# A sixth quartered tile in the first feed-forward's second product

## The chip, the cores and the metric

The kernel runs on one core of a Trainium2 chip. The metric is the device time of one execution in microseconds (us). Its engines run side by side and wait for one another through semaphores: PE (TensorE, matrix products, with its weight loads shown apart as PEld), DVE (VectorE), ACT (ScalarE), POOL (GpSimd) and SP (SyncE, which here only issues DMA transfers). In this program ACT, DVE, POOL and SP each go through their own list of instructions in the order in which it was written.

## The reference, cut to what matters

One decoder layer on 512 tokens of 1024 columns, in float32: a half-step feed-forward, a token mixer, and a second half-step feed-forward, each between two RMS norms.

```
x = x + 0.5 * rms_norm(swiglu_ffn(rms_norm(x, norm_pre[0]), ffn1_w_in, ffn1_w_out), norm_post[0])
mixed = token_mixer(rms_norm(x, norm_pre[1]), w_mix_in, ..., w_mix_out)
x = x + rms_norm(mixed, norm_post[1])
x = x + 0.5 * rms_norm(swiglu_ffn(rms_norm(x, norm_pre[2]), ffn2_w_in, ffn2_w_out), norm_post[2])

def swiglu_ffn(x, w_in, w_out):            # w_in 1024 x 5632, w_out 2816 x 1024
    gate, up = jnp.split(x @ w_in, 2, axis=-1)
    return (jax.nn.silu(gate) * up) @ w_out
```

The change lies in `(...) @ w_out` of the first feed-forward.

## The kernel before

**Products in three parts.** Each float32 operand is split into a high part (a cast on ACT, line 294 for weights, 884 for activations) and a low part (a subtraction on DVE, lines 296 and 885). A product is three matmuls: high by high, high by low, low by high.

**The second product.** `ffn_out` takes the 2816 rows of `w_out` in 11 tiles of 256 rows (`PAIRS = 11`), and the 1024 output columns in two halves. Per half it adds up in four PSUM banks `C[u][v]` (u: even or odd chunk of 128 tokens, v: 256 columns). A tile enters in one of two ways:

- plain (line 1004): 4 chunks of 128 tokens by 2 column halves by 6 matmuls, 48 matmuls of 128x256;
- by quarters (`quartered`, `product`, line 1012): a Strassen-Winograd form with 7 products of 6 matmuls, 42 in all. Three products go straight into `C`; four go into banks `M` that all quartered tiles of a half share. After the half's last quartered tile `common` forms four shared terms from `M` (one copy on ACT, line 1039, and four DVE operations), and `add` adds them to `C` (both on line 969).

A quartered tile needs more preparation: a second weight tile with sums of the four quarters, and sums of the quarters of the activations (`h_sums`, line 919, then split into a tile `hs`), besides the quarters' own parts (`h_quarters`, tiles `once` or `xq`). The sums of weights are not computed on an engine: `sums_ahead` copies quarters into a DRAM buffer `f1sums` by three DMAs on SP's queue (lines 938 to 940) and adds to them by three accumulating DMAs on POOL's queue (line 944), and a load reads the result. `make_sums` starts one such set and moves each begun set on by one step; `ffn_in`, the first product, calls it every fifth of its steps, and `ffn_out` on every other tile of the first half.

`QUARTERED` says which tiles are quartered in each half, `OUT` in which order a half takes its tiles, and `LAST` how many tiles at the end of the second half are held back: they are taken chunk by chunk (128 tokens at a time), so that the norm of a chunk can begin while the next is multiplied. In the second half of the first feed-forward that order is 10, 2, 4, 3, 6, 8, 9 and then, chunk by chunk, 0, 1, 7, 5.

```
FIRST = (2, 3, 4, 5, 6, 7, 8, 9)
OUT = {"f1": [list(range(PAIRS)), [10, 2, 4, 3, 6, 8, 9, 0, 1, 7, 5]]}
LAST, APART, TWICE = {"f1": 4, "f2": 2}, (5, 7, 9), (5, 9)
```

**Room.** Split weights have four places (`w`); a place is free when the last matmul of its tile has read it. Activations of this stage have three places (`hs`) and one more for tile 7 in `xq`. The quarters of tiles 5, 7 and 9 have no place of their own: their high part borrows a buffer of the ring `raw`, from which the mixer's first weights are loaded next, and their low part borrows `gpre`, the tile into which the pre-norm's gain for the mixer is loaded next (line 165).

**The end of the stage.** After a chunk's last matmul: `add` where it is due, squares and their sum on ACT (line 453), the root on POOL (lines 454 and 458), the scaling and the addition to `xs` on DVE (lines 501 and 509), then squares and root again for the mixer's norm, the scaling by `gpre` on DVE (line 481), and transposes on PE (line 364). `copies_early` also starts the copies of the second feed-forward's sums (`f2sums`, 7 sets of three DMAs on SP's queue). `head4` begins the mixer's first products (line 560).

**Order.** The program is written in the order of these functions; a scheduler then orders each engine's list by its own estimate of when things are ready.

Of the kernel before, what the change touches and what calls it, by code (L numbers as in the profile page):

```python
# [84 lines left out]


FIRST = (2, 3, 4, 5, 6, 7, 8, 9)
QUARTERED = {"f1": [FIRST, (2, 3, 4, 6, 8)], "f2": [FIRST, (2, 3, 4, 6, 8, 9, 5)]}
OUT = {"f1": [list(range(PAIRS)), [10, 2, 4, 3, 6, 8, 9, 0, 1, 7, 5]]}
OUT["f2"] = [OUT["f1"][0], [10, 2, 4, 3, 6, 8, 9, 5, 7, 0, 1]]  # L90
LAST, APART, TWICE = {"f1": 4, "f2": 2}, (5, 7, 9), (5, 9)
# [3 lines left out]
EVERY, EARLY, AHEAD = 5, 7, 13  # L95
# [28 lines left out]
class Layer:  # L124
    def __init__(self, ctx, tc, aps):
# [23 lines left out]
            (f, h, k2): dram.tile([P, 4, QUARTER], F32, name=f"{f}sums{h}_{k2}")  # L149
            for f in ("f1", "f2") for h in range(2) for k2 in OUT[f][h] if k2 in QUARTERED[f][h]  # L150
        }
# [691 lines left out]
    def ffn_in(self):  # L843

        nc = self.nc
        if not self.second:
            self.begun = ()
            self.sums_due("f1")
        for n, (p, t) in enumerate(ORDER2[len(HEADS2) :] if self.second else ORDER[len(HEADS) :]):
            if n > 14 and n % EVERY == 0 and not self.second:  # L850
                self.make_sums()
            if n == 14 and self.second:

                with self.behind(self.pooled):
                    nc.gpsimd.drain()
            with self.behind(*(self.c22 if p in ("p3", "p5") and self.second else ())):
                self.feed()
            self.c22 = []
            self.lag()
            self.prod(p, t)  # L860
            self.after(p, t)
            if t == PAIRS - 1 and p in ("p3", "p7"):
                self.hs.append(self.h_tile(len(self.hs)))
            if n == 1 and not self.second:
                self.lower_bound()
        self.feed()
        self.lag()
# [96 lines left out]
    def ffn_out(self, gpost_row, scale, after, trans, head):  # L964
# [5 lines left out]
        f = "f2" if self.second else "f1"  # L970
        OF, QF, LF = OUT[f], QUARTERED[f], LAST[f]
        low = self.low
# [234 lines left out]
    def ffn_items(self, name, w_in, w_out):  # L1207
# [47 lines left out]
        for h in range(2):  # L1255
            for k2 in OUT[name][h]:
                src = w_out[k2 * 2 * P : (k2 + 1) * 2 * P, h * 512 : (h + 1) * 512].rearrange("(k p) d -> p k d", p=P)
                key = (name, "out", h, k2)
                four = k2 in QUARTERED[name][h]
                made.append(Item(key, [Load(key, src, 2, 512, "raw2", 5, 8)], sums=four))  # L1260
# [717 lines left out]
```

## Time and profile before

| | us |
|---|---|
| median of 3 runs | 915.35 |
| lowest and highest | 915.20 and 915.37 |
| the profiled execution's own time | 916.13 |
| span in that profile, first to last instruction | 914.4 |
| PE busy in the span | 906.1 |
| DVE, ACT, POOL busy | 767.2, 522.0, 183.7 |

All times of places in the program below are counted from the span's start in the profiled execution. The second product of the first feed-forward lies between about 224 and 339 us; its second half of the columns begins at about 280 us. An engine's busy time says what it did, not whether it was waited for; that is read from the rows of single instructions, where a bracket gives the idle time ahead of an instruction and what ended it.

### The profile page before, as it was taken

To read this page: it belongs to the slowest core of one execution; us is meant where nothing else is said; L and a number is where in the kernel's file an instruction comes from. 1 tells how busy PE (TensorE), PEld (TensorE's weight loads), DVE (VectorE), ACT (ScalarE), POOL (GpSimd) and SP (SyncE) were. 2 spreads that over 40 slices of the span, in tenths; PEclk is the share of its full clock that TensorE was granted. 3 is DMA by queue.
4 is the path that set the end of the run, shared out by engine and by line. 5 is a ranking of instruction groups with operands and counts; after the bars stand their busy time and mean duration, and the time that the engine had idled before them with its cause. 6 is when DMAs were issued, how large, how long until landed. Compare 5 with 4: busy or idle time off the path is not lost.

```text
span 914.4 us, 18150 instructions
## 1 busy us (share of the span) xinstructions
PE 906.1 (99%) x7330; PEld 874.9 (96%) x7330; DVE 767.2 (84%) x1005; ACT 522.0 (57%) x749; POOL 183.7 (20%) x256
## 2 busy tenths in 40 slices
PE   9999999999999999999999999999999999999997
PEld 8999999999999999998888887899999999999997
DVE  6899988889888876799896556799999889998886
ACT  7645545557566567957643345684454545757661
POOL 2541112121111047742230300322000000010002
PEclk9999999999999999999999999999999999999999
DMA  9355779775897815898953126253344445378542
GB/s 306 88 165 136 189 188 216 187 159 138 219 280 233 258 55 144 162 192 207 214 112 109 47 70 213 65 161 102 97 148 139 138 123 159 104 231 246 170 146 93
DMA packets 127921, 146.51 MB, mean 160 GB/s; under 512 B 16335, under 2 KB 100303, under 8 KB 127837
## 3 DMA queue, kind: packets, MB, share of 16 engines
q1 hardware_dynamic: 111868, 130.14, 46.4%
q0 software_dynamic: 15680, 14.69, 11.9%
q8 instruction: 57, 0.93, 0.4%
q10 hardware_dynamic: 288, 0.52, 0.2%
q14 instruction: 28, 0.22, 0.1%
HBM read 143.20 MB, written 31.48 MB: 191 GB/s over the span
## 4 chain that ended last, share of the span: by engine, by line
PE 62%; ACT 0%; DVE 0%; DVEq 0%; POOLq 0%; issue 0%; POOL 0%; ACTq 0%
PE ps L619 23%; PE ps L1012 8%; PE ps L549 6%; PE ps L198 5%; PE ps L200 5%; PE ps L199 5%; PE ps L1004 4%; PE ps L560 1%; PE ps L1441 1%; PE ps L364 1%; PE ps L1540 0%; PE ps L1742 0%; PE ps L1491 0%; PE ps L1715 0%; PE ps L1739 0%; PE ps L1717 0%
## 5 line engine op out<-in xcount | busy, mean ns | idle before, releaser
L294 ACT CAST w<-raw 128x1024 fp32r<-128x1024 f32 x246 | 250.6, 1027 | 192.0 <-PE ps L619 91.1
L296 DVE TENSOR_TENSOR w<-raw,w 128x1024 fp32r<-128x1024 f32 x246 | 299.4, 1221 | 30.3 <-ACT w L294 28.9
L619 PE MATMUL ps<-xq,w 128*128 128x256 f32 x2016 | 237.4, 277 | 0.0
L619 PEld LDWEIGHTS ps<-xq,w 128*128 128x128 f32 x2016 | 233.3, 188 | 0.1
L619 PE MATMUL ps<-sq,w 128*128 128x256 f32 x1512 | 178.0, 276 | 0.0
L619 PEld LDWEIGHTS ps<-sq,w 128*128 128x128 f32 x1512 | 174.6, 188 | 0.0
L310 DVE TENSOR_TENSOR raw<-raw,raw 128x1024 f32<-128x1024 f32 x72 | 89.7, 1252 | 7.5 <-DMA raw<-in_ffn_w_in_dram 6.2
L1012 PE MATMUL ps<-w,hs 128*128 128x256 f32 x672 | 80.9, 276 | 0.0
L1004 PE MATMUL ps<-w,hs 128*128 128x256 f32 x672 | 79.2, 276 | 0.0
L1012 PEld LDWEIGHTS ps<-w,hs 128*128 128x128 f32 x672 | 78.3, 188 | 0.0
L1004 PEld LDWEIGHTS ps<-w,hs 128*128 128x128 f32 x672 | 77.5, 188 | 0.0
L198 PE MATMUL ps<-w,xq 128*128 128x512 f32 x176 | 71.1, 405 | 0.1
L199 PE MATMUL ps<-w,xq 128*128 128x512 f32 x176 | 68.6, 391 | 0.0
L200 PE MATMUL ps<-w,xq 128*128 128x512 f32 x176 | 68.6, 391 | 0.0
L549 PE MATMUL ps<-xq,w 128*128 128x256 f32 x480 | 55.7, 277 | 0.0
L944 POOL DMA_DIRECT2D f2sums<-in_ffn_w_out_dram x15 | 20.0, 1507 | 177.5 <-DMA f2sums<-in_ffn_w_out_dram 177.0
L549 PEld LDWEIGHTS ps<-xq,w 128*128 128x128 f32 x480 | 54.9, 188 | 0.5 <-issue 0.5
L884 ACT CAST hs<-hf 128x1024 fp32r<-128x1024 f32 x32 | 33.7, 1054 | 28.0 <-PE ps L1012 20.3
L885 DVE TENSOR_TENSOR hs<-hf,hs 128x1024 fp32r<-128x1024 f32 x32 | 39.1, 1223 | 9.0 <-ACT hs L884 8.4
L944 POOL DMA_DIRECT2D f1sums<-f1sums x26 | 22.3, 859 | 110.1 <-DMA f1sums<-in_ffn_w_out_dram 56.1
L944 POOL DMA_DIRECT2D f2sums<-f2sums x30 | 26.3, 905 | 87.1 <-DMA f2sums<-in_ffn_w_out_dram 42.4
L310 POOL TENSOR_TENSOR raw<-raw,raw 128x1024 f32<-128x1024 f32 x12 | 32.6, 2724 | 40.9 <-DVE w L296 40.7
(263 smaller groups left out, 1232.9 us busy)
## 6 DMA issues: line engine op xcount, KB each, us to landing
raw<-in_ffn_w_in_dram SPq DMA_DIRECT2D x98, 512.0 KB, 4.7
raw<-in_ffn_w_out_dram SPq DMA_DIRECT2D x44, 512.0 KB, 5.1
raw<-in_w_mix_in_dram SPq DMA_DIRECT2D x28, 512.0 KB, 5.7
raw<-f2sums SPq DMA_DIRECT2D x15, 512.0 KB, 5.2
raw<-f1sums SPq DMA_DIRECT2D x13, 512.0 KB, 7.0
raw<-in_w_mix_out_dram SPq DMA_DIRECT2D x8, 512.0 KB, 4.3
f2sums<-in_ffn_w_out_dram SPq DMA_DIRECT2D x30, 128.0 KB, 5.0
f2sums<-in_ffn_w_out_dram SPq DMA_DIRECT2D x15, 256.0 KB, 6.1
```

What stands on the lines that cost most here:

```text
L198: mm(ps, sh, mh, start=start, stop=False, **kw)
L199: mm(ps, sh, ml, start=False, stop=False, **kw)
L200: mm(ps, sl, mh, start=False, stop=stop, **kw)
L294: nc.scalar.copy(hi, raw)
L296: self.low = nc.vector.tensor_tensor(lo, raw, hi.bitcast(F32), op=ALU.subtract)
L310: added = (nc.vector if late else nc.gpsimd).tensor_tensor(o, o, c, op=ALU.add)
L549: mm(ps[:, u0:u1], w[:, a, k, :], self.xop(k, b, u0, u1), start=k + n + m == 0, stop=k == ND - 1 and n == 2, skip_group_check=True,)
L619: self.nc.tensor.matmul(ps[:, c], wb[b][:, k, v], left[d][:, k, :], start=first and a + n + k == 0, stop=n == 2 and k == KH - 1, skip_grou ...
L885: self.nc.vector.tensor_tensor(lo, src, hi.bitcast(F32), op=ALU.subtract)
L944: nc.gpsimd.dma_start(to[:, a:b], v, accum_op=ALU.add)
L1004: mm(out, a[kk][:, i * P : (i + 1) * P], w[:, b, kk, QUARTER * v : QUARTER * (v + 1)], start=begin and c == kk == n == 0, stop=kk == 1 and ...
L1012: mm(ps[:, QUARTER * c : QUARTER * (c + 1)], A[a][:, c], B[b], start=begin and c == n == 0, stop=n == 2, skip_group_check=True,)
```

## The change

```
-QUARTERED = {"f1": [FIRST, (2, 3, 4, 6, 8)], "f2": [FIRST, (2, 3, 4, 6, 8, 9, 5)]}
+QUARTERED = {"f1": [FIRST, (2, 3, 4, 6, 8, 9)], "f2": [FIRST, (2, 3, 4, 6, 8, 9, 5)]}
...
         for n, (p, t) in enumerate(ORDER2[len(HEADS2) :] if self.second else ORDER[len(HEADS) :]):
-            if n > 14 and n % EVERY == 0 and not self.second:
+            if n > 9 and n % EVERY == 0 and not self.second:
                 self.make_sums()
```

Tile 9 is taken by quarters in the second half of the columns too. With that no plain tile stands any more between the last quartered tile and the four that go chunk by chunk. Its sums of weights are a fourteenth set, and the first set is begun at step 10 of `ffn_in` and no longer at step 15. Since 9 is in `TWICE`, its quarters and sums are prepared anew for the second half, in borrowed places again.

PE, second half of the columns, tile 9 and what follows, before (`hs_3711` is tile 9, `hs_3767` tile 0; `ps_3441` and `ps_3442` are `C[0]`, `ps_3443` and `ps_3444` are `C[1]`):

```order
L1004 MATMUL ps_3441<-w,hs_3711 128x256 x6
L1004 MATMUL ps_3442<-w,hs_3711 128x256 x6
L1004 MATMUL ps_3441<-w,hs_3711 128x256 x6
L1004 MATMUL ps_3442<-w,hs_3711 128x256 x6
L1004 MATMUL ps_3443<-w,hs_3711 128x256 x6
L1004 MATMUL ps_3444<-w,hs_3711 128x256 x6
L1004 MATMUL ps_3443<-w,hs_3711 128x256 x6
L1004 MATMUL ps_3444<-w,hs_3711 128x256 x6
L1004 MATMUL ps_3441<-w,hs_3767 128x256 x6
```

And now, from the third of its seven products on (`once` is tile 9's quarters, `hs_3730` their sums, `hs_3779` tile 0; `ps_3508` to `ps_3510` are three of the banks `M`, `ps_3448` to `ps_3450` banks of `C`):

```order
L1012 MATMUL ps_3450<-w,hs_3730 128x256 x6
L1012 MATMUL ps_3509<-w,hs_3730 128x256 x6
L1012 MATMUL ps_3508<-w,hs_3730 128x256 x6
L1012 MATMUL ps_3510<-w,hs_3730 128x256 x6
L1012 MATMUL ps_3449<-w,once_3720 128x256 x2
L1012 MATMUL ps_3449<-w,once_3721 128x256
L1012 MATMUL ps_3449<-w,once_3720 128x256 x2
L1012 MATMUL ps_3449<-w,once_3721 128x256
L1004 MATMUL ps_3448<-w,hs_3779 128x256 x6
```

Eight groups of six became seven, and the banks `M` are complete only just ahead of tile 0.

DVE at the same place, before (the rows of line 969 are `common` and `add`; `raw_247` and `raw_249` are the weights of tiles 7 and 5, `hs_3774` and `hs_3779` the activations of tiles 1 and 5):

```order
L969 TENSOR_TENSOR hf_113<-ps_3501,hf_113 128x512
L885 TENSOR_TENSOR xq_77<-hf_113,xq_76 128x1024
L969 TENSOR_TENSOR hf_113<-ps_3503,hf_113 128x512
L296 TENSOR_TENSOR w<-raw_247_3634,w 128x1024
L969 TENSOR_TENSOR hf_113<-hf_113,ps_3502 128x512
L885 TENSOR_TENSOR hs_3774<-hf_113,hs_3774 128x1024
L969 TENSOR_TENSOR hf_113<-ps_3501,hf_113 128x512
L969 TENSOR_TENSOR ps_3443<-ps_3443,hf_113 128x512
L969 TENSOR_TENSOR ps_3444<-ps_3444,hf_113 128x512
L885 TENSOR_TENSOR hs_3779<-hf_113,hs_3779 128x1024
L296 TENSOR_TENSOR w<-raw_249_3665,w 128x1024
L969 TENSOR_TENSOR ps_3441<-ps_3441,hf_113 128x512
```

And now (`raw_249` and `raw_250` are the weights of tiles 7 and 5, `hs_3846` the activations of tile 5):

```order
L296 TENSOR_TENSOR w<-raw_249_3672,w 128x1024
L969 TENSOR_TENSOR hf_114<-ps_3508,hf_114 128x512
L969 TENSOR_TENSOR ps_3451<-ps_3451,hf_114 128x512
L969 TENSOR_TENSOR hf_114<-ps_3510,hf_114 128x512
L296 TENSOR_TENSOR w<-raw_250_3694,w 128x1024
L969 TENSOR_TENSOR hf_114<-hf_114,ps_3509 128x512
L885 TENSOR_TENSOR hs_3846<-hf_114,hs_3846 128x1024
L969 TENSOR_TENSOR hf_114<-ps_3508,hf_114 128x512
L969 TENSOR_TENSOR ps_3450<-ps_3450,hf_114 128x512
L969 TENSOR_TENSOR ps_3448<-ps_3448,hf_114 128x512
```

All of line 969 now stands behind the weights of tile 7, and the low part of tile 5's activations stands inside it.

SP's queue, before, where the gain for the mixer's norm is loaded (`gpre`):

```order
L255 DMA raw_191_3290<-f1sums_3_92 128x1024
L255 DMA raw_3736<-in_w_mix_in_dram 128x8x128
L165 DMA gpre_3923<-in_norm_pre_dram 128x1024
L255 DMA raw_196_3327<-in_ffn_w_out_dram 128x2x512
L255 DMA raw_234_3447<-f1sums_6_93 128x1024
```

And now, behind the 21 copies for the second feed-forward, of which these are the last:

```order
L255 DMA raw_3839<-in_w_mix_in_dram 128x8x128
L940 DMA f2sums_6_100<-in_ffn_w_out_dram 128x512
L938 DMA f2sums_7_101<-in_ffn_w_out_dram 128x256
L939 DMA f2sums_7_101<-in_ffn_w_out_dram 128x256
L940 DMA f2sums_7_101<-in_ffn_w_out_dram 128x512
L938 DMA f2sums_8_102<-in_ffn_w_out_dram 128x256
L939 DMA f2sums_8_102<-in_ffn_w_out_dram 128x256
L940 DMA f2sums_8_102<-in_ffn_w_out_dram 128x512
L165 DMA gpre_3938<-in_norm_pre_dram 128x1024
L255 DMA raw_4216<-in_w_mix_in_dram 128x8x128
```

The gain's load went from ahead of all `f2sums` copies to behind all of them, and one load of the mixer's weights went in between them. The sums of tile 9 make one weight load more ahead of the copies.

## Prediction

> **What bounds the kernel now.** I read the page's first part, then busy time by stretch, then PE's waits, then single instructions around the stage's end.
>
> ```profile
> span 914.4 us, 18150 instructions
> PE 906.1 (99%) x7330; PEld 874.9 (96%) x7330; DVE 767.2 (84%) x1005; ACT 522.0 (57%) x749; POOL 183.7 (20%) x256
> ```
>
> PE is busy for 906.1 of 914.4 us, so time is won or lost in PE's work and in PE's few waits. The stretches of the second half of the columns (five quartered tiles, the plain tile 9, the chunks), with PE, PEld, DVE, ACT, POOL in this order:
>
> ```profile
> 285.66:309.46 23.80, 23.80 (x213) 23.80 (x211) 17.37 (x17) 16.44 (x18) 0.00 (x0) 1.00 0.76 235
> 309.46:314.90 5.44, 5.44 (x51) 5.44 (x49) 5.44 (x7) 1.52 (x2) 0.00 (x0) 1.00 0.92 246
> 314.90:336.60 21.70, 21.70 (x193) 21.70 (x192) 15.25 (x25) 10.41 (x29) 6.84 (x17) 1.00 0.34 95
> ```
>
> PE has no gap. DVE is idle for 6.4 us over the five quartered tiles, but never in the 5.44 us of tile 9. PE's matmuls there, and its next wait:
>
> ```profile
> 301.30 2.88 PE L1012 MATMUL ps<-w,hs 128*128 128x256 f32 x24
> 306.06 2.88 PE L1012 MATMUL ps<-w,hs 128*128 128x256 f32 x24
> 309.46 8.32 PE L1004 MATMUL ps<-w,hs 128*128 128x256 f32 x72
> 317.62 1.52 PE L1004 MATMUL ps<-w,xq 128*128 128x256 f32 x12
> 338.79 5.53 PEld L560 LDWEIGHTS ps<-xq,w 128*128 128x128 f32 x48 [0.29 <-ACT w L294]
> ```
>
> From one row to the same place of the next tile a quartered tile takes 306.06 - 301.30 = 4.76 us, and 72 plain matmuls take 317.62 - 309.46 = 8.16 us, 113.3 ns each. PE then runs without a stop up to 338.5, where the mixer's first product waits 0.29 us for a weight cast on ACT. That wait has a history, and it decides this change. The chain of waits ends there with
>
> ```profile
> 336.35 0.47 ACT junk L453 x2
> 336.83 0.96 ACT xq L370 x2
> 337.79 0.95 ACT w L294
> 338.79 5.73 PE ps L560 x48
> ```
>
> and going back from 336.35 instruction by instruction I find no slack:
>
> ```profile
> 319.86 1.38 DVE L969 TENSOR_TENSOR ps<-ps,hf 128x512 f32<-128x512 f32 x2 [1.31 <-PE ps L1004]
> 322.94 0.75 DVE L509 SCALAR_TENSOR_TENSOR xs<-y,col,xs 128x512 f32<-128x512 f32 x1 [0.66 <-POOL col L458]
> 323.79 0.63 ACT L453 ACTIVATE junk<-xs 128x512 f32<-128x512 f32 x1 [1.96 <-DVE xs L509]
> 326.42 1.43 DVE L481 SCALAR_TENSOR_TENSOR xn<-xs,col,gpre 128x512 f32<-128x512 f32 x2 [2.06 <-POOL col L458]
> 329.26 0.64 ACT L453 ACTIVATE junk<-xs 128x512 f32<-128x512 f32 x1 [2.73 <-DVE xs L509]
> 331.89 1.43 DVE L481 SCALAR_TENSOR_TENSOR hf<-xs,col,gpre 128x512 f32<-128x512 f32 x2 [2.06 <-POOL col L458]
> 334.74 0.63 ACT L453 ACTIVATE junk<-xs 128x512 f32<-128x512 f32 x1 [1.80 <-DVE xs L509]
> ```
>
> Each step starts when the one before ends: the addition to `C[0]` at 319.86 lets the first chunk's norm begin; that ends in the scaling by `gpre` at 326.42; behind it on DVE stands the second chunk's addition, whose norm scales at 331.89; behind that the third chunk's, whose squares at 334.74 hold ACT until 336.35. So from 319.86 to 338.79 there is a second path beside PE's, of 18.93 us, and at 338.79 it is the later one by 0.29 us. The stage ends when the addition at 319.86 starts, plus 18.93, unless something delays the chain.
>
> **The change part by part.** *PE's work.* Tile 9 goes from 48 to 42 matmuls: 6 x 113.3 ns = 0.68 us less (5.44 to 4.76). This is the whole possible gain; it brings tile 0 from 314.90 to 314.22.
>
> *When the addition to `C[0]` now starts.* It stands on DVE behind the rest of `common`. The durations and distances come from
>
> ```profile
> 309.76 1.22 DVE L885 TENSOR_TENSOR xq<-hf,xq 128x1024 fp32r<-128x1024 f32 x1
> 310.90 0.68 DVE L969 TENSOR_TENSOR hf<-ps,hf 128x512 f32<-128x512 f32 x1
> 311.50 1.22 DVE L296 TENSOR_TENSOR w<-raw,w 128x1024 fp32r<-128x1024 f32 x1
> 315.10 1.06 ACT L884 CAST hs<-hf 128x1024 fp32r<-128x1024 f32 x1 [4.12 <-PE ps L1004]
> 316.06 1.04 ACT L294 CAST w<-raw 128x1024 fp32r<-128x1024 f32 x1
> ```
>
> A low part of 1024 lets the next start after 1.14, one of line 969 after 0.60; ACT starts 0.20 after PE frees a place (315.10 after 314.90). Tile 9's first weight place is free after 18 matmuls, at 311.50: ACT casts tile 7's weights from 311.70 to 312.75, DVE takes their low part at 312.78. Then 313.92 and three rows of line 969 up to 315.72. Tile 9's sums are read after 36 matmuls (313.54), its second weights at 314.22; ACT casts tile 5's activations 313.74 to 314.80 and its weights 314.70 to 315.75. DVE: their low part at 315.78, line 969 at 316.92, the activations' low part at 317.52 (done 318.74), line 969 at 318.66 and 319.26, and the addition to `C[0]` at 319.86. PE reaches tile 5 in the first chunk at 314.22 + 3 x 1.36 = 318.30 and needs that low part in its third matmul, so it waits some 0.4 us for 318.74; the matmuls that the addition needs end near 319.4, ahead of 319.86. PE would leave the first chunk at 320.05, where it was 320.34.
>
> So PE arrives 0.3 us earlier, but the addition starts at the same 319.86 as before. By the chain the stage ends at 338.79 again, PE waits 0.6 us there in place of 0.3, and the gain is gone: 0.0, with -0.3 if the chain starts that much earlier than I count and -0.68 at most.
>
> *The load of `gpre`.* It was far ahead; now it waits for tile 9 (its buffer) and stands behind the copies. It is needed at 326.42, on the chain without slack.
>
> ```profile
> 275.27 1.58 SPq L165 DMA_DIRECT2D gpre<-in_norm_pre_dram  x1
> 302.93 2.22 SPq L255 DMA_DIRECT2D raw<-in_ffn_w_out_dram  x1
> 305.20 0.51 SPq L938 DMA_DIRECT2D f2sums<-in_ffn_w_out_dram  x1
> 318.76 0.60 SPq L940 DMA_DIRECT2D f2sums<-in_ffn_w_out_dram  x1
> DMA to landing us min/median/max: 4.4/5.1/5.4
> DMA to landing us min/median/max: 3.8/3.8/3.8
> DMA to landing us min/median/max: 7.1/7.1/7.1
> ```
>
> (The landings are those of the `f2sums` copies, of the one load of a gain that the trace shows landing, and of a load of mixer weights at 300 us.) The copies took the queue from 305.20 to 319.36. Now two issues more stand ahead or among them; an issue takes 0.3 to 0.6 when the queue flows and 1.6 to 2.2 behind other large loads, so `gpre` is issued between 320.0 and 323. It lands 3.8 to 7.1 later. Ends: 323.8, which costs nothing, and 330.1, which costs 3.7. I take 321.3 + 5.4, the slowest copy, because it moves among copies: 326.7, late by 0.3.
>
> The Trainium skill, "DMA: Bandwidth & Descriptors", section "Queues, rings and completion order", says that each DMA engine consumes the descriptors of a ring in order. By it `gpre` cannot overtake the eight last copies; by the 3.8 us of a gain's load alone it would land at 325.1 and cost nothing, by the rule at 326.7 or later. No row here shows a load among copies landing early.
>
> *More work for DVE and ACT*: the quarters' low parts, three sums and one more split of 768 columns. The same operations for other tiles:
>
> ```profile
> 246.05 0.69 DVE L919 TENSOR_TENSOR hsum<-hf,hsum 128x512 f32<-128x512 f32 x1
> 257.49 1.02 DVE L885 TENSOR_TENSOR once<-hf,once 128x256 fp32r<-128x256 f32 x2
> 298.42 0.96 DVE L296 TENSOR_TENSOR w<-raw,w 128x768 fp32r<-128x768 f32 x1 [0.27 <-ACT w L294]
> 255.00:300.00 45.00, 45.00 (x399) 45.00 (x399) 37.43 (x47) 29.84 (x47) 6.32 (x13) 1.00 0.85 252
> ```
>
> At most 3 x 0.69 + 1.02 + 0.96 = 4.1 us of DVE, ahead of 305, where DVE is idle for 45 - 37.4 = 7.6 us between 255 and 300: 0. Without that cover it would delay the splits of weights behind it one for one.
>
> *The sums begun earlier.* SP's queue gets three issues more behind 65.83:
>
> ```profile
> 65.83 0.53 SPq L255 DMA_DIRECT2D raw<-in_ffn_w_in_dram  x1
> 75.09 4.97 SPq L255 DMA_DIRECT2D raw<-in_ffn_w_in_dram  x2
> ```
>
> Between them the queue waits for a buffer for 8.7 us; three issues take under 2. All later sets keep the places that other sets had, and the fourteenth ends where the thirteenth did: 0, and 2 at most if the weights behind came late.
>
> Sum: -0.68 (PE) + 0.4 (tile 5) + 0.3 (chain takes the rest) + 0.3 (`gpre`) = +0.3. The profiled execution took 916.13, 0.78 above the median; the difference is applied to the median: 915.35 + 0.3 = 915.65, say 915.7.
>
> **The rivals.** *The gain arrives.* If tile 5's weights or activations are ready earlier, or the addition overtakes, PE keeps 0.3 to 0.68: 914.7 to 915.05. Against it: DVE's continuous row from 312.78 to 319.86.
>
> *`gpre` is late in earnest.* One mechanism, at 326.42: each us of landing after it is a us of time. From 328.25 on (7 us after an issue at 321.3) it makes the kernel slower by over 0.2%: 916.4 to 919. For it: DMA is busy 0.92 in tile 9's stretch and gets three loads more; against it: the copies' landing never exceeds 5.4.
>
> *A stopped PE runs slower afterwards.* The granted clock is 1.00 around the 0.29 us wait:
>
> ```profile
> 338.50:340.00 1.50, 1.41 (x12) 1.21 (x12) 1.35 (x3) 1.42 (x4) 0.54 (x1) 1.00 0.00 0
> ```
>
> With `gpre` at 330.1 PE would stand 0.6 + 3.7 us at 338; if its 48 matmuls of 5.73 us then ran at half speed, 5.7 more: up to 924.8. The Trainium skill, "TensorE: Matmul & The Clock Gate", section "HAM oscillation — how this bites in real kernels", warns of idle gaps above some 3.4 us. No wait here is that long, so the trace cannot confirm it.
>
> *The early sums disturb* the first product's weights: 915.7 to 917.4.
>
> **How the numbers follow.** Chain-bound with `gpre` at most 1 us late: 0.62 (915.2 to 916.4). The gain arrives: 0.15. `gpre` over 1 us late: 0.19, most of it over 1.83. Clock: 0.02. Early sums: 0.02. About 0.2% (1.83 us) is what a measurement of this kernel can tell from no change. Slower by more: 0.13 + 0.02 + 0.01 = 0.16; faster by more: 0.01, since PE's whole saving is 0.68; within: 0.83. The range, 914.9 to 917.5, leaves out the full gain and the latest landings; the likeliest case alone is 915.2 to 916.4.
>
> **What would show it.** Right: 42 matmuls for tile 9 in 4.76 us; a wait of about 0.4 at tile 5 of the first chunk; line 969 on `C[0]` at 319.9; line 481 at 326.4 to 327.4, ended by POOL or by the load of `gpre`; PE's wait at 338.5 of 0.6 us or more. Wrong: line 969 clearly before 319.6 or after 320.5; PE starting the mixer before 338.5; a PE gap between 60 and 280.

## The result and the profile after

The changed kernel takes 920.02 us in the median of 7 runs (919.11 to 925.47), the kernel before 915.37 (915.20 to 915.49): a ratio of 1.0066, with a 95% interval from 1.0053 to 1.0080. It is slower by 4.65 us, and it lies outside the range that was given, 914.9 to 917.5. The seven executions fall into two groups: four between 919.1 and 920.0 and three between 923.6 and 925.5. The profiled one, 919.99 us by its own time, is of the first group.

The page's first part, after:

```profile
span 918.3 us, 18165 instructions
PE 906.7 (99%) x7324; PEld 874.8 (95%) x7324; DVE 770.6 (84%) x1011; ACT 524.0 (57%) x752; POOL 185.9 (20%) x259
```

PE executes 7324 matmuls where it had 7330, six fewer as intended, and yet is busy 0.6 us longer; the span is 3.9 us longer. So PE's work cannot be the whole story: PE waits more, and somewhere its matmuls run slower. PE's waits behind 300 us say where:

```profile
PE ps L560 <- ACT w L294: 2.0, 1, 2.0
PE ps L364 <- DVE hf L481: 0.9, 1, 0.9
PE ps L1004 <- DVE hs L885: 0.2, 1, 0.2
```

Of these, before had only the first, with 0.29 us. Row by row on PE (start, duration, group, and in brackets the idle time ahead and its releaser):

```profile
308.98 1.52 PE L1012 MATMUL ps<-w,once 128*128 128x256 f32 x12
310.34 2.88 PE L1012 MATMUL ps<-w,hs 128*128 128x256 f32 x24
313.74 2.88 PE L1004 MATMUL ps<-w,hs 128*128 128x256 f32 x24
318.42 2.90 PE L1004 MATMUL ps<-w,hs 128*128 128x256 f32 x23 [0.21 <-DVE hs L885]
341.36 7.35 PE L560 MATMUL ps<-xq,w 128*128 128x256 f32 x48 [2.02 <-ACT w L294]
348.55 1.03 PE L364 MATMUL ps<-ident,xn 128*128 128x128 f32 x8
```

Tile 9 begins at 308.98 here (309.46 before: this execution came 0.48 us earlier into the stage) and takes 313.74 - 308.98 = 4.76 us. The 48 first matmuls of the mixer, 5.73 us before, now take 7.35. What PE waited for, on DVE and on SP's queue:

```profile
318.88 1.89 DVE L969 TENSOR_TENSOR ps<-ps,hf 128x512 f32<-128x512 f32 x3
329.00 1.41 DVE L481 SCALAR_TENSOR_TENSOR xn<-xs,col,gpre 128x512 f32<-128x512 f32 x2 [5.12 <-DMA gpre<-in_norm_pre_dram]
305.44 0.51 SPq L938 DMA_DIRECT2D f2sums<-in_ffn_w_out_dram  x1
320.56 0.60 SPq L940 DMA_DIRECT2D f2sums<-in_ffn_w_out_dram  x1
321.72 0.35 SPq L165 DMA_DIRECT2D gpre<-in_norm_pre_dram  x1
```

The scaling by `gpre`, which POOL used to release, is released by the load. The load was issued behind the copies of `f2sums` (305.44 to 321.16) and the scaling starts 7.28 us after its issue. The granted clock, the last column but two of these stretches, is 1.00 up to 342 and then:

```profile
342.00:344.00 2.00, 2.00 (x12) 2.00 (x12) 1.89 (x4) 1.56 (x2) 1.56 (x2) 0.53 0.09 14
344.00:346.00 2.00, 2.00 (x13) 2.00 (x13) 2.00 (x3) 1.48 (x3) 0.66 (x1) 0.61 0.86 248
346.00:348.00 2.00, 2.00 (x20) 2.00 (x20) 2.00 (x3) 1.75 (x4) 1.30 (x2) 1.00 0.25 34
```

PE was busy throughout these rows, with 12 or 13 matmuls in 2 us instead of 20: it did not wait there, it ran at a lower clock. In stretches of 0.2 us the granted clock reads 0.50 from 342.2 to 345.4 and 1.00 again from 345.6 on: some 3.4 us at half clock.

**A ruler for this stage.** Executions enter the stage some tenths of a us apart, so below I measure from the start of tile 9. *Scaling* is the time from there to the first line 481; *stage* is the time to the transposes (line 364) that follow the mixer's first 48 matmuls. Before, the latter stand at

```profile
344.36 1.03 PE L364 MATMUL ps<-ident,xn 128*128 128x128 f32 x8
```

so that before has a scaling of 326.42 - 309.46 = 16.96 and a stage of 344.36 - 309.46 = 34.90. After has 329.00 - 308.98 = 20.02 and 348.55 - 308.98 = 39.57: the scaling is 3.06 us late, the stage 4.67, and 4.67 - 3.06 = 1.61 is the matmuls at lower clock (7.35 - 5.73 = 1.62).

### The profile page after: what moved, and what is told of

Its sections match the earlier page's. It is cut to its first block, busy times and chain, and to the rows that moved or that the text cites. A ratio compares the mean times of both kernels' runs of the same rounds, so it can differ in the third digit from the quotient of the medians.

```text
span 918.3 us, 18165 instructions
## 1 busy us (share of the span) xinstructions
PE 906.7 (99%) x7324; PEld 874.8 (95%) x7324; DVE 770.6 (84%) x1011; ACT 524.0 (57%) x752; POOL 185.9 (20%) x259
## 4 chain that ended last, share of the span: by engine, by line
PE 62%; ACT 0%; issue 0%; DVE 0%; DVEq 0%; POOLq 0%; POOL 0%; ACTq 0%
PE ps L619 23%; PE ps L1012 8%; PE ps L549 6%; PE ps L198 5%; PE ps L200 5%; PE ps L199 5%; PE ps L1004 4%; PE ps L560 1%; PE ps L1441 1%; PE ps L364 1%; PE ps L1540 0%; PE ps L1742 0%; PE ps L1491 0%; PE ps L1715 0%; PE ps L1739 0%; PE ps L1717 0%
## 5 line engine op out<-in xcount | busy, mean ns | idle before, releaser
L294 ACT CAST w<-raw 128x1024 fp32r<-128x1024 f32 (+1 forms) x247 | 251.6, 1027 | 192.4 <-PE ps L619 90.8
L296 DVE TENSOR_TENSOR w<-raw,w 128x1024 fp32r<-128x1024 f32 (+1 forms) x247 | 300.3, 1220 | 29.3 <-ACT w L294 27.8
L1012 PE MATMUL ps<-w,hs 128*128 128x256 f32 x696 | 83.8, 276 | 0.0
L1012 PEld LDWEIGHTS ps<-w,hs 128*128 128x128 f32 x696 | 81.1, 188 | 0.0
L1004 PE MATMUL ps<-w,hs 128*128 128x256 f32 x624 | 74.0, 277 | 0.2 <-DVE hs L885 0.2
L1004 PEld LDWEIGHTS ps<-w,hs 128*128 128x128 f32 x624 | 72.2, 188 | 0.4 <-DVE hs L885 0.4
L944 POOL DMA_DIRECT2D f1sums<-f1sums x28 | 24.7, 883 | 113.9 <-DMA f1sums<-in_ffn_w_out_dram 56.8
```

The source lines that it names most:

```text
L294: nc.scalar.copy(hi, raw)
L296: self.low = nc.vector.tensor_tensor(lo, raw, hi.bitcast(F32), op=ALU.subtract)
L944: nc.gpsimd.dma_start(to[:, a:b], v, accum_op=ALU.add)
L1004: mm(out, a[kk][:, i * P : (i + 1) * P], w[:, b, kk, QUARTER * v : QUARTER * (v + 1)], start=begin and c == kk == n == 0, stop=kk == 1 and ...
L1012: mm(ps[:, QUARTER * c : QUARTER * (c + 1)], A[a][:, c], B[b], start=begin and c == n == 0, stop=n == 2, skip_group_check=True,)
```

## The experiments

Each ratio below compares with executions of the kernel before in the same series; their medians lay between 915.61 and 915.85.

**The early sums alone.** The kernel before, with the second part of the change only:

```
-            if n > 14 and n % EVERY == 0 and not self.second:
+            if n > 9 and n % EVERY == 0 and not self.second:
```

> The kernel before with the first set of sums begun at step 10 of the first product; tile 9 stays plain in the second half. Theory (the late gain load, then the slowed clock): this edit has no part in the loss, 915.2 to 915.6. Rival (the sums begun earlier disturb the weight loads of the first product): 917 to 920, with PE gaps between 60 and 225 us.

Measured: 915.73 us (915.31 to 916.49), ratio 0.9998 [0.9989, 1.0007]. The stage is 34.91 us. The sums begun earlier have no part in it.

**The late load alone.** The kernel before, tile 9 plain, with the load of `gpre` forced behind the last copy, and nine sets of copies ahead of it instead of seven:

```
-EVERY, EARLY, AHEAD = 5, 7, 13
+EVERY, EARLY, AHEAD = 5, 9, 13
...
+        last = self.copies_last if tag == "gpre" else None
+        with self.behind(*([last] if last else [])):
             self.nc.sync.dma_start(g, row.broadcast_to([P, D]))
```

> The kernel before, tile 9 plain, with only the load of the mixer's gain moved behind the copies of the second feed-forward's sums; nine sets of copies stand ahead of it in place of seven, so that it is issued near 323 us and lands near 328.0 to 329.5, where it is needed at 326.4. Theory: the load alone makes the loss: the scaling by the gain starts 1.6 to 3.1 us late, PE stands 1.9 to 3.4 us ahead of the mixer's first product, and where the clock falls after that another 1.6: 917 to 920. Rival (the quartered tile, with common close to the chunks, makes the loss): 915.4, no wait for the gain or one that costs nothing.

Measured: 921.72 us (921.44 to 922.55), ratio 1.0062 [1.0050, 1.0074]. The rows of SP, DVE and PE:

```profile
324.88 0.59 SPq L168 DMA_DIRECT2D gpre<-in_norm_pre_dram  x1
332.75 1.41 DVE L485 SCALAR_TENSOR_TENSOR xn<-xs,col,gpre 128x512 f32<-128x512 f32 x2 [7.84 <-DMA gpre<-in_norm_pre_dram]
345.10 5.16 PE L564 MATMUL ps<-xq,w 128*128 128x256 f32 x43 [2.02 <-ACT w L298]
```

Without any change to tile 9, the late load alone makes a loss of this kind, and here a larger one. It landed later than expected: the scaling starts 7.87 us after the issue, 22.74 us after tile 9's start (310.01), which is 5.78 late, and the time grew by 5.9. (PE's first 43 matmuls ran here at full speed, although it had waited 2.02 us ahead of them and 1.71 and 1.25 before.)

**The load ahead of the copies.** The changed kernel; the load is issued before `copies_early`, whose copies then stand behind it:

```
+            self.gpre1 = self.gain("gpre", self.norm_pre[0][1:2, :])
             self.copies_early()
...
-        w, last = (self.ffn1_w_out, self.ffn2_w_out)[f == "f2"][0], self.loaded1 if early else self.loaded
+        w, last = (self.ffn1_w_out, self.ffn2_w_out)[f == "f2"][0], self.gained if early else self.loaded
```

> The changed kernel with the gain's load moved ahead of the copies: it waits for tile 9 at 314 us and the 21 copies wait behind it. Theory: the gain lands near 320, the scaling by it waits for POOL again, PE's wait ahead of the mixer is some 0.6 us and the clock stays at 1.00: 915.0 to 915.6, since the norm's chain starts where it did before. Rival (the quartered tile makes the loss): 919 to 920 as before.

Measured: 921.13 us in the median, but in two groups: 915.75 to 916.90 (5 executions) and 921.05 to 923.40 (7); ratio 1.0041 [1.0022, 1.0060]. The profiled execution (916.90) is of the first group. In it the stage is whole again:

```profile
315.59 0.53 SPq L165 DMA_DIRECT2D gpre<-in_norm_pre_dram  x1
327.25 1.43 DVE L481 SCALAR_TENSOR_TENSOR xn<-xs,col,gpre 128x512 f32<-128x512 f32 x2 [2.06 <-POOL col L458]
339.62 5.72 PE L560 MATMUL ps<-xq,w 128*128 128x256 f32 x48 [0.27 <-ACT w L294]
```

POOL releases the scaling again; tile 9 began at 310.29, so the scaling is 16.96 and the stage 34.89, the values of before. So the late load, with the fall of the clock behind it, is the whole loss inside the stage, and there is a second loss of some 6 us elsewhere, in seven of the twelve executions.

**A place of its own for tile 9's quarters**, so that `gpre` is not borrowed and is loaded as early as before (line numbers are one higher in this kernel):

```
-                        a = self.h_quarters(k2, PLACES.get(k2))
+                        a = self.h_quarters(k2, AGAIN9 if half and k2 == 9 and not self.second else PLACES.get(k2))
```

with `AGAIN9 = 1`, a place in `xq`.

> The changed kernel with tile 9's quarters of the second half in the place that tile 2 leaves at 290 us, and not in the buffers of the gain and of the mixer's weights: both loads go back to where they stood in the kernel before. Theory: 914.9 to 915.5; PE does 0.68 us less, the addition to C[0] starts where it did, and the norm's chain takes the rest. If the chain were not binding: 914.7. Rival (the quartered tile makes the loss): 919 to 920.

Measured: 916.61 us (915.34 to 922.89; two of twelve at 922.9, the others up to 917.17), above the 914.9 to 915.5 expected; ratio 1.0017 [1.0001, 1.0033]. Load issued at 275.35, scaling 16.96, stage 34.90. The quarters are there, all 42 matmuls, and yet the stage is not shorter by a hundredth.

**The wait filled.** The changed kernel with 12 transposes (1.47 us in its profile) ahead of the mixer's first product, into a bank that it overwrites:

```
+        if t + m == 0:
+            for _ in range(FILLERS):
+                self.nc.tensor.transpose(ps[:, :P], self.ident, self.ident)
```

> The changed kernel, with 12 transposes of the identity (about 1.8 us) ahead of the mixer's first product, into the bank that this product then overwrites. They fill PE's wait of 2.02 us there and change nothing else; the gain's load stays late. Theory (the late load starts it, and the wait of 2.02 us then halves the granted clock, 1.62 us): the wait is covered but for 0.2 us, the clock stays 1.00 from 341 on, the first 48 matmuls of the mixer take 5.7 us again, and the time falls by about 1.6 us, to 918.4. Rival (the slow matmuls have another cause, such as the 0.85 us wait six us earlier, or a fixed rhythm): the clock falls all the same, and the time stays at 920.

Measured: 918.6 us (917.48 to 924.56), ratio 1.0042 [1.0023, 1.0062]; four executions at 917.5 to 918.1, two at 922.9 and 924.6, two between. The profiled execution (920.37) had a later load than after (scaling 20.67, 3.71 late), a stage 3.70 longer, and a clock of 1.00 throughout: the loss is the lateness alone. That speaks for the wait as the cause of the slow matmuls, but it does not prove it, since `b_gain_late` kept its clock without any filling; and the second group blurs the median.

**Fewer copies ahead of the load.** The changed kernel with four sets instead of seven:

```
-EVERY, EARLY, AHEAD = 5, 7, 13
+EVERY, EARLY, AHEAD = 5, 4, 13
```

> The changed kernel with 4 sets of copies for the second feed-forward's sums ahead of the gain's load instead of 7 (12 transfers instead of 21); the other three are made later, in the mixer. Theory (the gain's landing is set by the transfers queued ahead of it): it is issued near 316.5, lands at 322 to 324, before it is needed at 326.4; the scaling ends its wait on POOL again, the mixer's first product on 0.3 us; 915.2 to 916. Rival (each load of the gain that is issued in this stretch takes 10 us and more, whatever stands ahead): still late by 0.5 us or more and 916.5 to 918. If the three sets moved into the mixer cost something there: 1 us more in either case.

Measured: 938.10 us (936.76 to 940.29), ratio 1.0246 [1.0232, 1.0259]: neither theory's number. In the stage it is as the first one had it:

```profile
316.06 0.96 SPq L165 DMA_DIRECT2D gpre<-in_norm_pre_dram  x1
326.39 1.43 DVE L481 SCALAR_TENSOR_TENSOR xn<-xs,col,gpre 128x512 f32<-128x512 f32 x2 [2.06 <-POOL col L458]
338.77 5.71 PE L560 MATMUL ps<-xq,w 128*128 128x256 f32 x48 [0.30 <-ACT w L294]
```

Scaling 16.98, stage 34.91. But the three sets that are now made in the mixer cost there what my expectation had put at 1 us:

```profile
502.06 0.81 POOL L944 DMA_DIRECT2D f2sums<-f2sums  x1 [2.59 <-DMA f2sums<-f2sums]
502.61 1.51 POOL L1624 TENSOR_SCALAR_AFFINE_SELECT e<-e 128x512 f32<-128x512 f32 x2
503.56 1.29 DVE L1634 SCALAR_TENSOR_TENSOR pT<-ps,e 128x512 f32<-128x512 f32 x2 [25.21 <-POOL e L1624]
504.31 1.54 PE L1672 MATMUL ps<-ident,qk 128*128 128x128 f32 x6 [19.48 <-DVE pT L1634]
```

This is a place that the prediction had left out. In the mixer POOL issues the accumulating transfers of `f2sums` (line 944), and most of them wait for the landing of an earlier transfer. Behind that row, on the same engine, stands the selection of line 1624 for the mixer's scores. DVE needs it for line 1634, and PE's line 1672 waits for that. With three sets more the row ends at 502.6, and PE stands for 19.48 us. Here, where PE stood waiting for it, line 1672 started 1.70 us after the selection, so a distance of 1.7 us means no margin. Before, it started 12.0 us after it:

```profile
472.09 0.81 POOL L944 DMA_DIRECT2D f2sums<-f2sums  x1 [3.11 <-DMA f2sums<-f2sums]
472.69 1.51 POOL L1624 TENSOR_SCALAR_AFFINE_SELECT e<-e 128x512 f32<-128x512 f32 x2
484.69 0.87 PE L1672 MATMUL ps<-ident,qk 128*128 128x128 f32 x6
```

By this distance the other profiles read: `a_sums_early` 11.1, after 10.1, `d_own_place` 5.4, `e_filled_wait` 1.7, and `c_gain_first` 1.8:

```profile
483.86 1.51 POOL L1625 TENSOR_SCALAR_AFFINE_SELECT e<-e 128x512 f32<-128x512 f32 x2
485.62 1.09 PE L1673 MATMUL ps<-ident,qk 128*128 128x128 f32 x6
```

Leave aside this kernel and `b_gain_late`, whose five executions lie close together (921.4 to 922.6). Then each kernel so far with executions above 922 is one whose selection started 5.4 us or less ahead of line 1672 in a profile (the changed kernel in its second profile, below).

**After, and the load ahead of the copies, once more for their traces.** No edit in either.

> The changed kernel once more, for its trace. Its times lay at 919 to 920 and at 923.6 to 925.5. Theory: an execution of the second kind has the same late load and, on top of it, a longer stretch at half clock or a later stop at another place, which the trace then shows as 4 to 5 us. Rival: the load itself lands 4 us later in it.

> The changed kernel with the gain's load ahead of the copies once more, for its trace. Its times lay at 915.8 to 916.9 and at 921 to 923.4. Theory: an execution of the second kind has a stop of PE at a place behind 340 us (a weight or a sum that comes late because the copies were moved back by the load), 2 to 6 us with the clock's part. Rival: no new stop, and PE runs at a lower granted clock from some place on.

Measured: 919.46 us and 915.84 us, one run each; neither fell into the second group, so no trace of that group was seen. The second execution of the changed kernel is worth having all the same:

```profile
323.93 0.35 SPq L165 DMA_DIRECT2D gpre<-in_norm_pre_dram  x1
329.80 1.41 DVE L481 SCALAR_TENSOR_TENSOR xn<-xs,col,gpre 128x512 f32<-128x512 f32 x2 [4.90 <-DMA gpre<-in_norm_pre_dram]
342.16 5.73 PE L560 MATMUL ps<-xq,w 128*128 128x256 f32 x48 [2.00 <-ACT w L294]
342.00:344.00 2.00, 1.84 (x16) 1.84 (x17) 1.86 (x3) 2.00 (x5) 1.26 (x2) 1.00 0.00 0
486.45 1.51 POOL L1624 TENSOR_SCALAR_AFFINE_SELECT e<-e 128x512 f32<-128x512 f32 x2
488.17 1.13 PE L1672 MATMUL ps<-ident,qk 128*128 128x128 f32 x6
```

The same wait of 2.0 us as in the first execution, but no fall of the clock: scaling 2.85 late, stage 2.84 longer. And the distance from selection to line 1672, 10.1 in the first execution, is 1.7 in this one: in the same kernel POOL's row, from its first issue to its last, took 103.8 us in one execution and 110.9 in the other. In the second execution with the load ahead of the copies the distance was 2.1 us.

**A shorter row.** The changed kernel, with one set of sums less in the mixer (`AHEAD` 12 instead of 13), and then the same with tile 9's place of its own:

```
-EVERY, EARLY, AHEAD = 5, 7, 13
+EVERY, EARLY, AHEAD = 5, 7, 12
```

> The changed kernel with one set of sums for the second feed-forward less in the mixer (12 instead of 13 done by its end; the thirteenth is made in the second feed-forward). POOL's row of accumulating transfers in the mixer, behind which its selection for the mLSTM scores stands (line 1624), becomes three transfers shorter, about 10 us. Theory (two costs: the late load of the gain, 3 to 4 us in every execution; and in some executions POOL's row reaching past the point where PE needs the scores, 3 to 6 us more): the selection stands 10 us or more ahead of PE's line 1672 again, the executions at 923 to 925 are gone, and all lie at 918.5 to 920.5. Rival (the second group comes from somewhere else): times up to 925 remain.

> The changed kernel with tile 9's quarters in the place of their own (so that the gain's load is early again) and with 12 instead of 13 sets done by the mixer's end. Theory of two costs: both are gone; all executions lie at 915.0 to 916.0 against 915.4 to 915.9 of before, none above 917. Rival (the quarters' 0.68 us do arrive once both are gone): 914.7 to 915.2. Rival (something else of the change costs as well): 916.4 or more.

Measured for the first: 920.39 us (918.25 to 921.17, 6 executions), ratio 1.0046 [1.0033, 1.0059]. The distance is 19.5 us, and nothing lies above 921.2 (918.5 to 920.5 was expected). In the profiled one the scaling is 2.42 late, the stage 4.03 longer; the clock fell again, and 1.61 us are its part, as in the first profile of after:

```profile
341.37 7.35 PE L560 MATMUL ps<-xq,w 128*128 128x256 f32 x48 [2.01 <-ACT w L294]
```

Measured for the second: 915.96 us (915.54 to 918.20, 11 executions), ratio 1.0008 [1.0000, 1.0017]; the distance is 15.9 us and nothing lies at 922 any more. None above 917 was expected; three lie at 917.5 to 918.2, where before had one of 17, at 918.4.

```profile
326.50 1.43 DVE L482 SCALAR_TENSOR_TENSOR xn<-xs,col,gpre 128x512 f32<-128x512 f32 x2 [2.07 <-POOL col L459]
338.88 5.71 PE L561 MATMUL ps<-xq,w 128*128 128x256 f32 x48 [0.30 <-ACT w L295]
344.43 1.03 PE L365 MATMUL ps<-ident,xn 128*128 128x128 f32 x8
```

Tile 9 began at 309.52: scaling 16.98, stage 34.91. With both costs removed the change stands where before stood, 0.2 us above it by the medians. No kernel that was run beats the kernel before.

**Fewer copies and a shorter row.** The changed kernel with `EARLY` 4 and `AHEAD` 10, so that the mixer makes six sets as before. In it the last two sets of sums for the second feed-forward are not completed, so nothing behind 700 us, and no time of the whole, says anything about the change.

> The changed kernel with 4 sets of copies ahead of the gain's load instead of 7, and 10 sets instead of 13 done by the mixer's end, so that the mixer makes six sets as before. Theory: the gain is issued 5 us earlier and lands before 326.4, POOL's row in the mixer ends early, and the time is 915.0 to 916.2 without any change to the places of buffers. Rival (the borrowed buffer costs by itself, whatever is queued): 917 or more, with the scaling of line 481 still ended by the load. If the five sets made late hold up the second feed-forward: a PE wait behind 760 us.

Measured: 921.98 us (918.80 to 924.34), with a PE wait in the second feed-forward,

```profile
PE ps L1012 <- DVE y L491: 3.7, 1, 3.7
```

as the third clause had it. From 300 to 700 us PE waits only 0.3 and 0.2: the load, issued at 317.06, is in time (scaling released by POOL, 16.96), though the buffer is still borrowed. What counts is what is queued ahead of the load.

**A shorter row, and the wait filled**, with 16 transposes.

> The changed kernel with 12 sets done by the mixer's end, as in i_short_row, and with 16 transposes of the identity (about 1.9 us) ahead of the mixer's first product. With POOL's row short, only the late load of the gain and what follows PE's 2.0 us wait are left; the transposes fill that wait. In i_short_row the profiled execution had a granted clock of 0.58 and 0.57 from 342 to 346 and the times lay at 918.25 to 921.17. Theory (the wait halves the clock in most executions, 1.6 us): the clock stays 1.00 there, and the times gather at 917.5 to 918.8, their median 1.5 to 2 us under 920.4. Rival (the spread comes from when the load lands, and the clock only follows): the median stays at 920 or above, with PE's wait behind the transposes up to 2 us.

Measured: 919.37 us (918.06 to 921.48, 5 executions), ratio 1.0037 [1.0023, 1.0051]. The median is 1.0 under `i_short_row`, less than the 1.5 to 2 expected. The mean granted clock is 0.998 or 0.999 in all five executions, and 0.996 to 0.999 in the six without the transposes. In the profile:

```profile
330.04 1.42 DVE L482 SCALAR_TENSOR_TENSOR xn<-xs,col,gpre 128x512 f32<-128x512 f32 x2 [5.33 <-DMA gpre<-in_norm_pre_dram]
342.39 5.73 PE L564 MATMUL ps<-xq,w 128*128 128x256 f32 x48 [0.26 <-ACT w L295]
```

Scaling 3.29 late, stage 3.27 longer, clock 1.00. So the rival had a part of it: what remains in this stage is the lateness of the load. But only 3.3 of the 5.3 us by which this profile's span is longer than before's lie there. From the last transposes before the second feed-forward (598.82 here, 595.07 before) to the end it took 320.9 us, before 319.3. From that place `j_both` took 319.6 and `i_short_row` 320.1, also with `AHEAD` 12; the ten profiles with 13 took 318.5 to 319.3. So the shorter row seems to have a price of its own, 0.3 to 1.6 us above before: the set that is moved into the second feed-forward is the likely reason, which no run isolates.

## Why the prediction was wrong, step by step

**The load of `gpre` was mis-sized.** This is the step that failed. It was named, it was put on the right chain, and its place behind the copies was right; its size was not. In time from tile 9's start the prediction had the issue at 11.84 (321.3) and the landing 5.4 later, 17.24, late by 0.3. The five profiles with tile 9's quarters in the borrowed buffer and seven sets of copies ahead:

| profile | issue | issue to scaling | scaling late | stage longer | rest |
|---|---|---|---|---|---|
| predicted | 11.84 | 5.4 | 0.3 | | |
| after | 12.74 | 7.28 | 3.06 | 4.67 | 1.61 |
| after, again | 13.94 | 5.87 | 2.85 | 2.84 | -0.01 |
| `i_short_row` | 12.83 | 6.55 | 2.42 | 4.03 | 1.61 |
| `e_filled_wait` | 13.18 | 7.49 | 3.71 | 3.70 | -0.01 |
| `l_short_filled` | 13.28 | 6.97 | 3.29 | 3.27 | -0.02 |

The issue came 0.9 to 2.1 us later than taken and the landing 0.5 to 2.1: the two errors add. The lateness stayed inside the bound that the prediction had set, 3.7, to a hundredth (single issues came 0.4 later and landings 0.4 longer than its ends of 323 and 7.1, never both), but the middle was taken from the fastest neighbours: 5.4 was the slowest of *small* copies (128 and 256 KB), while the 512 KB load that it showed beside them had 7.1 (two others, issued at 278.4 and 294.5 us, took 6.7 and 5.0). And with the change the copies land later themselves. Those of `f2sums`, 4.4, 5.1 and 5.4 before, are now at

```profile
DMA to landing us min/median/max: 4.3/5.6/6.8
```

so that the argument against the rival, that no copy takes over 5.4 us, did not carry over to the changed kernel. The rival "late in earnest" had a chance of 0.19 and the prices 916.4 to 919; it is what happened, with the clock's loss on top. The prediction had cited, in the Trainium skill, "DMA: Bandwidth & Descriptors", section "Queues, rings and completion order", that a ring's descriptors are taken in order. No run here shows that order itself. What they show is that the load, issued behind 21 copies, took 5.9 to 7.5 us until its reader started and was late, and that behind 12 copies it was issued 5.5 to 7.3 us earlier and was in time.

**The clock was given 0.02.** In two of three profiles with an unfilled wait of 2.0 us on the changed code, the 48 matmuls behind it took 7.35 us instead of 5.73: 1.6 us. The prediction priced 5.7 us for a stop of over 4 us. The section "HAM oscillation — how this bites in real kernels" of the page "TensorE: Matmul & The Clock Gate" in the Trainium skill warns of gaps above some 3.4 us; the measurement differs, since here the clock fell behind a wait of 2.0 us, with 0.2 or 0.9 us more six us earlier. With the wait filled the clock stayed at 1.00 in both profiles; since it stayed there in two of four without filling as well, the wait is the likely cause and not a proven one, and why the same wait is followed by a fall in one execution and not in another stays open.

**The row on POOL was not seen.** The prediction placed the early sums' cost between 60 and 280 us and the copies' cost at `gpre`; it did not follow the sums into the mixer. That a longer row stops PE at line 1672 is shown (`f_fewer_ahead`, 19.48 us). That it makes the executions at 923 to 925 is likely, not shown: with the row shortened none of 22 executions (`i_short_row`, `j_both`, `l_short_filled`) lay above 921.5, against 3 of 7 (after), 5 of 12 (`c_gain_first`, whose second group has two more at 921.1 and 921.2), 2 of 12 (`d_own_place`) and 2 of 8 (`e_filled_wait`) with the row as it was, but no trace caught one. The mean granted clock of each execution says a little more: it is 0.998 in the five of `c_gain_first`'s first group and 0.994 to 0.996 in the seven of its second. Of some 920 us that is about 2 to 4 us (an estimate), so part of the 6 us seems to be a lower clock. Why the row ends later with the change than without it (12.0 and 11.1 us ahead of PE against 10.1, 5.4, 2.1, 1.8 and 1.7) stays open: the order on POOL is the same, and the same 39 transfers took 101.5 and 102.3 us without the change and 103.8 to 112.0 in six profiles with it.

**What held.** Tile 9 took 4.76 us with 42 matmuls, as computed. The addition to `C[0]` was put at 319.86, and starts at 319.48 here (0.60 after 318.88), 319.96 when shifted by 0.48. The wait at tile 5 of the first chunk, put at 0.4, is 0.21 in its bracket, but by the starts of the rows it cost 0.50: from tile 5 in the first chunk up to the second row of tile 7 behind it, 48 matmuls, PE took 324.42 - 318.98 = 5.44 us before and 323.76 - 317.82 = 5.94 after.

```profile
318.98 2.88 PE L1004 MATMUL ps<-w,hs 128*128 128x256 f32 x24
324.42 0.84 PE L1004 MATMUL ps<-w,xq 128*128 128x256 f32 x6
317.82 0.39 PE L1004 MATMUL ps<-w,hs 128*128 128x256 f32 x2
323.76 0.84 PE L1004 MATMUL ps<-w,xq 128*128 128x256 f32 x6
```

(The first two rows are of before, the others of after.) In `c_gain_first`, with the load in time, the same stretch takes 5.94 us too and the mixer's first product starts 0.18 us later behind the last matmuls than before: -0.68 + 0.50 + 0.18 = 0.0, where the prediction had 0.4 and 0.3. The early sums cost nothing by themselves. Above all, the reading that the gain is swallowed by the chain behind that addition held to a hundredth: wherever `gpre` was in time, the stage took 34.89 to 34.92 us with tile 9 plain or by quarters, but for one profile at 35.09 (`k_fewer_both`). With the load in time and POOL's row short the kernel is where `j_both` is, 0.24 us above the 915.72 of before in its series, where the prediction had 0.3. With the load in time alone it stood at 916.6 (`d_own_place`) or in two groups (`c_gain_first`): what lies behind the second group was missing from the prediction too.

**The sum as it was.** In the profiled execution +3.06 (load) + 1.61 (clock) = 4.67 us in the stage. It had entered the stage 0.48 earlier than the one before, which leaves 4.2, and 0.3 came back behind the stage: the span grew by 3.9. The median grew by 4.65, since three of the seven executions lie in the second group.

## What to carry to other kernels

A buffer that is borrowed just before a load ties the load's issue to the borrower's last reader, and in a queue written in program order that means behind everything issued in between; price such a load by the slowest row of its own size in the busiest stretch, and add the delay of the issue and that of the landing. Ahead of saving an engine's work, look for a second path that ends within that saving: here PE already waited 0.29 us for the chain at the stage's end, so that none of its 0.68 us could arrive. When transfers on an engine's queue wait for one another, look at which computation stands behind the row, since its margin can be gone long before a trace shows a wait.

## What the runs showed of the hardware

- A TensorE wait of 2.0 us was followed by about 3.4 us at half clock (0.53 and 0.61, 0.58 and 0.57 in stretches of 2 us) in two profiles, and by none in two others with the same wait (`g_after_again`, `b_gain_late`).
- A load of 512 KB issued behind 21 copies from DRAM to DRAM took 5.9 to 7.5 us until its reader started, and behind 27 copies 7.9; the one load of a gain that the trace of before shows landing took 3.8.
- The same row of 39 accumulating transfers on POOL, most of them waiting for earlier transfers, took 101.5 us before, and 103.8 and 110.9 in two executions of the changed kernel.
